# Input projections as seven-product Strassen blocks over even and odd tokens, and a 31-tap convolution as three half-rate filters, in a two-layer fp32 trunk

## The chip, the cores and the metric

One core of one Trainium2 chip runs the whole program. The metric is the device time of one execution in microseconds. The core's engines run side by side: TensorE (PE; its weight loads are shown as PEld), VectorE (DVE), ScalarE (ACT) and GpSimd (POOL). SyncE (SP) issues every transfer, in one queue, in the order in which the instructions stand there.

## What is computed

`SEQ` is 2048 tokens, `D_MODEL` 1024 channels, everything fp32. Layer 0 has mixer A, layer 1 mixer B.

```python
for l in range(DEPTH):                       # DEPTH = 2
    mod = cond @ ada_w[l] + ada_b[l]         # shift, scale, gate from silu(c)
    u = x * (1.0 + scale) + shift
    if l == 0:                               # mixer A
        a, g, z = split(u @ a_w_in + a_b_in, 3)           # 1024 -> 3072
        h = causal_depthwise_conv_31(a * sigmoid(g)) + a_conv_b
        h = silu(layer_norm_over_channels(h))
        y = (h * silu(z)) @ a_w_out + a_b_out
    else:                                    # mixer B
        bg, cg, v, z = split(u @ b_w_in, 4)               # 1024 -> 4096
        y = (bg * causal_depthwise_conv_3(cg * v) * silu(z)) @ b_w_out
    x = layer_norm(ALPHA * x + gate * y) * post_ln_g[l] + post_ln_b[l]
```

## The kernel before

**Tiling.** The tokens are four quarters of T = 512, the channels K = 8 blocks of 128. A projection's result is a PSUM bank of 128 channels by 512 tokens. Each fp32 product is made of three matmuls on rounded parts (hi by hi, hi by lo, lo by hi; L138 to L140 in `products`, L310 to L312 in `mixer_out`), so one output block of one quarter costs 8 x 3 matmuls. There are 24 such blocks for layer A's input projection, 32 for layer B's and 16 for the two output projections: 72 x 24 x 4 = 6912 matmuls of 512 columns. Beside them stand 416 128x128 transposes: of x on the way in (L168), of the convolution's result for its channel statistics (L511), and of layer A's output.

**Weights.** `weight` (L112) loads a block raw (512 KB, L83, on SP), ScalarE copies the hi part (L117), GpSimd subtracts to get the lo part (`wi_lo`, `wb_lo`, `wo_lo`, L119, 1024 elements a partition). This is done again for each of the four quarters. `fold_gate` (L246) multiplies the output weights by the gate row once (L271) and stores them (L272).

**Convolution.** `conv_a` (L389) works on one block of 128 channels and one quarter, as two chains of taps on VectorE, each with its own PSUM bank (`pca`, `pcb`; L412); the few leading taps are on ScalarE and GpSimd, L422 adds the chains. The taps stand in a list, `todo`, of which the main program issues some after every projection block.

**Layer B's middle.** `gated_b` (L595) multiplies two banks (L601), does the three taps (L607, L609), and gates (L611, L613).

**Order.** A table of numbers, `SCH`, sets how the quarters interleave: the projection of a quarter's layer B runs beside the statistics, the norm (`a_norm`, L548 to L555) and the output projection of the next quarter's layer A. The taps of the convolution are thus spread over about three quarters of the program. Inside what the numbers fix, a scheduler places instructions on each engine; matmuls of one block stay together. Of other lines that are named later, L218 sums the modulation rows from `ada_w`, L319 takes an output projection out of PSUM and adds the residual, L514 and L516 gather statistics, L456 is the GLU product on GpSimd, L455 copies a halo, and L464 stores z.

Of the kernel before, what the change touches and what calls it, by code (L numbers as in the profile page):

```python
# [9 lines left out]
F32 = mybir.dt.float32  # L10
# [9 lines left out]
K = D // P  # L20
T = 512
# [3 lines left out]
KB = 3  # L25
DEPTH = 2
ALPHA = (2.0 * DEPTH) ** 0.25
EPS = 1e-5
BOOST = 600
EXTRA = {3: (3,)}  # L30
BUFS = dict(raw=2, whi=3, wlo=3, uh=9, ul=9, xk=2, uf=2, big=28, h=5, ta=4, tv=5, zz=2, xr=4)
BANKS = dict(mm=4, tp=2, conv=2)
MAIN = ("raw", "whi", "wlo")
SPARE = ("raw", "xr", "xr")
SCH = dict(f0=4, p1=21, a1=5, n0=9, b0=20, bq=17, nq=10, pb=0, pa=16, ra=7, rb=4, rc=11, g0=3, w0=1, bt=600, ev=2, x4=3, io=0, c0=1, cq=0, pj=1, k1=1, k2=5, gb=0, gk=0, vv=0, a0=2, wm=0, rr=1, pk=6, ay=5, wq=1, lk=1, z1=3, zq=0, mo=0, m0=0)
# [3 lines left out]
def hybrid_trunk(ctx, tc, x, c, ada_w, ada_b, a_w_in, a_b_in, a_conv_w, a_conv_b,  # L39
                 a_ln_g, a_ln_b, a_w_out, a_b_out, b_w_in, b_conv_w, b_w_out,  # L40
                 post_ln_g, post_ln_b, out):
    nc = tc.nc
# [10 lines left out]
    def bank(tag, name):  # L53
        return psum.tile([P, T], F32, tag=tag, bufs=BANKS[tag], name=name)


# [5 lines left out]
    nc.gpsimd.memset(mhalf, -0.5)  # L62

    rows = []
# [9 lines left out]
              ("pg0", cols(post_ln_g[0]), K),  # L74
              ("pb0", cols(post_ln_b[0]), K),
# [3 lines left out]

    in_order = [bool(SCH["io"])]  # L80

    def load(dst, src):
        ins = nc.sync.dma_start(dst, src)  # L83
        if in_order[0]:
            tc.keep_in_program_order(ins)

    def load_columns(gi, g):
        n = sum(r[2] for r in g)
        rt = st("ta", [P, P], f"rt{gi}")
# [5 lines left out]
        nc.tensor.transpose(pt[:, :n], rt[:n, :], ident[:n, :n])  # L95
        ct = const.tile([P, n], F32, name=f"cols{gi}")
        nc.vector.tensor_copy(ct, pt[:, :n])
        o = 0
        for key, ap, m in g:
            col[key] = ct[:, o:o + m]  # L100
            o += m

    load_columns(0, first)
# [3 lines left out]
    def wa_col(k, e):  # L107
        i = k * K + e
        return col["wa0"][:, i:i + 1] if i < half else col["wa1"][:, i - half:i - half + 1]


    def weight(src, name, tags=MAIN):  # L112

        raw = st(tags[0], list(src.shape), name + "_raw")
        load(raw, src)
        hi = st(tags[1], list(src.shape), name + "_hi", F32R)
        nc.scalar.copy(hi, raw)  # L117
        lo = st(tags[2], list(src.shape), name + "_lo", F32R)
        nc.gpsimd.tensor_tensor(lo, raw, hi.bitcast(F32), op=ALU.subtract)  # L119
        return hi, lo  # L120

    def weight_in(w, m, e, name, **kw):
        o = m * D + e * P
        hi, lo = weight(w[:, o:o + P].rearrange("(k p) j -> p k j", p=P), name, **kw)
        return [hi[:, k] for k in range(K)], [lo[:, k] for k in range(K)]

    beside = deque()

    def products(pss, ws, acts):

        behind = None
        for k in range(K):
            ah, al = acts[k]
            with ExitStack() as order:
                if behind is not None:
                    order.enter_context(tc.issue_after(behind))
# [4 lines left out]
            behind = None  # L141
            if beside and len(pss) == 1 and k % SCH["ev"] == SCH["ev"] - 1:
                with tc.issue_after(mm.ins):
                    behind = beside.popleft()()

    def split(full, tagh, tagl, name, eng):
        hi = st(tagh, [P, T], name + "h", F32R)
        lo = st(tagl, [P, T], name + "l", F32R)
        nc.scalar.copy(hi, full)
        eng.tensor_tensor(lo, full, hi.bitcast(F32), op=ALU.subtract)  # L150
        return hi, lo

    su1 = const.tile([P, K], F32, name="su1")
    bu1 = const.tile([P, K], F32, name="bu1")

    w_dram = [dram.tile([2, K // 2, P, 2, T], F32, name="w_dram0"),
              dram.tile([2, K // 2, P, 2, T], F32, name="w_dram1")]
    z_dram = dram.tile([NQ, K, P, T], F32, name="z_dram")
    n_dram = dram.tile([S, D], F32, name="n_dram")

    def prep_k(q, l, k, src, su, bu, tag="xk"):

        xk = st(tag, [P, NT, P], f"xk{l}_{q}_{k}")
        load(
            xk, src[q * T:(q + 1) * T, k * P:(k + 1) * P].rearrange("(t p) j -> p t j", p=P))
        pt = bank("tp", f"ptx{l}_{q}_{k}")
        for t in range(NT):
            nc.tensor.transpose(pt[:, t * P:(t + 1) * P], xk[:, t, :], ident)  # L168
# [13 lines left out]
    def normalise(dst, src, rs, mv, name):  # L182
# [3 lines left out]
        for d, s in zip(dst, src):  # L186
            nc.scalar.activation(d, s, AF.Identity, scale=rs, bias=nb)

    def ada_sum(l, m, h, res, shared=0):

# [541 lines left out]
```

## Time and profile before

| what | value |
|---|---|
| time, median of 3 executions | 1740.15 us (1736.21 to 1741.71) |
| the profiled execution: its time, its span | 1741.81 us, 1740.0 us |
| TensorE busy | 1669.4 us, 96% of the span |
| VectorE busy | 1313.7 us, 76% |
| GpSimd busy | 1114.6 us, 64% |
| ScalarE busy | 636.1 us, 37% |
| moved by DMA | 265.27 MB, mean 152 GB/s |

The time is taken by the device; the span goes from the first to the last instruction of the profile. The shares are averages over stages that look different: VectorE, at 76% on average, is at 98% in some stretches. Mean durations hide a spread where an instruction waits for something inside itself, so three views are used: the groups of instructions by line with their mean, the single lines with minimum, median and maximum, and windows of time with the busy time of every engine.

### The profile page before, as it was taken

What the parts mean: (1) busy time and instruction counts of PE and PEld (TensorE: products, weight loads), DVE (VectorE), ACT (ScalarE), POOL (GpSimd) and SP (SyncE); (2) the same over time, 40 slices, a digit from 0 to 9 for tenths busy, and PEclk for the clock granted to TensorE, in tenths of its full rate; (3) what the DMA queues carried; (4) which work ended last, traced back from release to release, by engine and by line L of the source; (5) the groups of instructions that cost most, each with busy time, mean ns of one, the idle gap of its engine ahead of it and who ended that gap; (6) DMA issues with size and microseconds to landing.
All of it is one profiled execution on the core that took longest, in us unless ns stands there. A gap on an engine that the chain in (4) does not pass through costs nothing.

```text
span 1740.0 us, 20572 instructions
## 1 busy us (share of the span) xinstructions
PE 1669.4 (96%) x7468; PEld 1371.9 (79%) x7468; DVE 1313.7 (76%) x1748; ACT 636.1 (37%) x820; POOL 1114.6 (64%) x710
## 2 busy tenths in 40 slices
PE   6999899889999999999999999999999999999997
PEld 4788688677788787888888787888888778888886
DVE  8999999899996545899994736599995736444464
ACT  2444545534223442435322434344422414222221
POOL 3798558876775876656554857655644777654444
PEclk9999999889999999999999999999999999999999
DMA  9965435766653564533432554543333436443342
GB/s 253 292 208 184 125 99 188 262 215 176 219 192 116 175 214 125 168 115 113 115 97 85 176 183 150 173 124 109 103 97 98 145 109 219 125 137 97 97 140 82
DMA packets 332053, 265.27 MB, mean 152 GB/s; under 512 B 10536, under 2 KB 289456, under 8 KB 331952
## 3 DMA queue, kind: packets, MB, share of 16 engines
q1 hardware_dynamic: 331952, 263.96, 48.5%
q8 instruction: 59, 0.97, 0.2%
q14 instruction: 42, 0.34, 0.1%
HBM read 230.36 MB, written 33.55 MB: 152 GB/s over the span
## 4 chain that ended last, share of the span: by engine, by line
PE 72%; DVE 11%; POOL 5%; DMA 5%; issue 4%; ACT 2%; SPq 1%; POOLq 0%; DVEq 0%; ACTq 0%
PE pq L138 11%; PE pq L139 11%; PE pq L140 11%; PE pi L139 7%; PE pi L140 7%; PE pi L138 7%; PE po L311 5%; PE po L312 5%; PE po L310 5%; POOL wi_lo L119 1%; DVE pca L412 1%; DVE v L555 1%; DVE pcb L412 1%; PE ptx L168 1%; DVE acc L548 1%
## 5 line engine op out<-in xcount | busy, mean ns | idle before, releaser
L119 POOL TENSOR_TENSOR wb_lo<-wb_raw,wb_hi 128x1024 fp32r<-128x1024 f32 x128 | 312.6, 2445 | 202.1 <-ACT wb_hi L117 173.6
L119 POOL TENSOR_TENSOR wi_lo<-wi_raw,wi_hi 128x1024 fp32r<-128x1024 f32 x96 | 232.9, 2428 | 158.0 <-ACT wi_hi L117 147.5
L412 DVE SCALAR_TENSOR_TENSOR pca<-h,cols,pca 128x512 f32<-128x512 f32 x440 | 328.3, 746 | 1.3
L412 DVE SCALAR_TENSOR_TENSOR pcb<-h,cols,pcb 128x512 f32<-128x512 f32 x416 | 310.0, 745 | 25.5 <-ACT pcb L400 25.2
L117 ACT CAST wb_hi<-wb_raw 128x1024 fp32r<-128x1024 f32 x128 | 134.5, 1051 | 392.3 <-PE pq L139 217.4
L119 POOL TENSOR_TENSOR wo_lo<-wo_raw,wo_hi 128x1024 fp32r<-128x1024 f32 (+1 forms) x65 | 165.7, 2551 | 77.8 <-ACT wo_hi L117 68.5
L117 ACT CAST wi_hi<-wi_raw 128x1024 fp32r<-128x1024 f32 x96 | 100.5, 1048 | 237.6 <-PE pi L139 105.0
L319 DVE TENSOR_TENSOR r<-po,r 128x512 f32<-128x512 f32 x64 | 43.4, 681 | 187.0 <-PE po L312 186.9
L117 ACT CAST wo_hi<-wo_raw 128x1024 fp32r<-128x1024 f32 (+1 forms) x65 | 67.3, 1037 | 151.6 <-PE po L312 74.8
L609 DVE SCALAR_TENSOR_TENSOR cc<-hb,cols,cc 128x512 f32<-128x512 f32 x64 | 95.3, 1489 | 1.1
L601 DVE TENSOR_TENSOR hb<-pq,cv 128x512 f32<-128x512 f32 x32 | 21.9, 686 | 66.0 <-PE pq L140 63.4
L611 DVE TENSOR_TENSOR cc<-cc,szb 128x512 f32<-128x512 f32 x32 | 55.7, 1740 | 15.8 <-ACT szb L605 15.2
L168 PE MATMUL ptx<-ident,xk 128*128 128x128 f32 x256 | 40.3, 290 | 16.7 <-ACT uf L170 7.5
L168 PEld LDWEIGHTS ptx<-ident,xk 128*128 128x128 f32 x256 | 32.9, 150 | 24.4 <-ACT uf L170 8.1
L138 PE MATMUL pq<-u_0h,wb_hi 128*128 128x512 f32 x128 | 50.7, 396 | 0.7 <-ACT szb L605 0.7
L218 DVE SCALAR_TENSOR_TENSOR ada<-adaw,cond,ada 128x512 f32<-128x512 f32 x32 | 48.7, 1522 | 2.5 <-DMA adaw<-in_ada_w_dram 2.1
L140 PE MATMUL pq<-u_0h,wb_lo 128*128 128x512 f32 x128 | 50.4, 394 | 0.0
L139 PE MATMUL pq<-u_0l,wb_hi 128*128 128x512 f32 x128 | 50.4, 393 | 0.0
L138 PE MATMUL pq<-u_7h,wb_hi 128*128 128x512 f32 x128 | 50.3, 400 | 0.0
L139 PE MATMUL pq<-u_2l,wb_hi 128*128 128x512 f32 x128 | 50.1, 392 | 0.0
L139 PE MATMUL pq<-u_7l,wb_hi 128*128 128x512 f32 x128 | 50.1, 392 | 0.0
L138 PE MATMUL pq<-u_1h,wb_hi 128*128 128x512 f32 x128 | 50.1, 391 | 0.0
(373 smaller groups left out, 5086.7 us busy)
## 6 DMA issues: line engine op xcount, KB each, us to landing
wb_raw<-in_b_w_in_dram SPq DMA_DIRECT2D x128, 512.0 KB
wi_raw<-in_a_w_in_dram SPq DMA_DIRECT2D x96, 512.0 KB
wo_raw<-w_dram SPq DMA_DIRECT2D x63, 512.0 KB
adaw<-in_ada_w_dram SPq DMA_DIRECT2D x60, 256.0 KB
adak<-in_ada_w_dram SPq DMA_DIRECT2D x32, 256.0 KB
xk<-in_x_dram SPq DMA_DIRECT2D x32, 256.0 KB
z_dram<-zv SPq DMA_DIRECT2D x32, 256.0 KB
zz<-z_dram SPq DMA_DIRECT2D x32, 256.0 KB
```

The lines of the kernel that those rows point to most:

```text
L117: nc.scalar.copy(hi, raw)
L119: nc.gpsimd.tensor_tensor(lo, raw, hi.bitcast(F32), op=ALU.subtract)
L138: nc.tensor.matmul(ps, hi[k], ah, start=(k == 0), stop=False)
L139: nc.tensor.matmul(ps, hi[k], al, start=False, stop=False)
L140: mm = nc.tensor.matmul(ps, lo[k], ah, start=False, stop=(k == K - 1))
L168: nc.tensor.transpose(pt[:, t * P:(t + 1) * P], xk[:, t, :], ident)
L310: nc.tensor.matmul(pss[t], gh[:, sl], hi, start=(k == 0), stop=False)
L311: nc.tensor.matmul(pss[t], gh[:, sl], lo, start=False, stop=False)
L312: nc.tensor.matmul(pss[t], gl[:, sl], hi, start=False, stop=(k == K - 1))
L412: nc.vector.scalar_tensor_tensor(out=ts[dst], in0=h[:, k:k + T], scalar=wa_col(k, e), in1=ts[src], op0=ALU.mult, op1=ALU.add)
L609: nc.vector.scalar_tensor_tensor(out=cc, in0=hb[:, k:k + T], scalar=wbc(k), in1=cc, op0=ALU.mult, op1=ALU.add)
L611: nc.vector.tensor_tensor(cc, cc, sz, op=ALU.mult)
```

## The change

**Strassen blocks.** The two halves of the sequence (`sc` 0 and 1, 1024 tokens each) take the place of the quarters in both input projections. A half is seen as two streams of 512, the even and the odd tokens (`hf` 0 and 1); quarter q is now 2 x half + parity. A `Pair` takes two 128-wide output blocks, the four even and the four odd blocks of the contraction, and the two streams: a 2x2 by 2x2 block product, made with seven block products (`PARTS`) where eight stood. Each is 4 x 3 matmuls. They gather in three PSUM banks (x, y, z); the bank x runs through four of the parts and is read in between. Layer A has 12 pairs, layer B 16, each in two halves: (12 + 16) x 7 x 12 x 2 = 4704 matmuls, and with the 1536 of the output projections 6240.

**Sums around the products.** VectorE forms the differences of the streams (`u_second`, L220: t1 to t4, four subtractions for each pair of contraction blocks, and three of their four lo parts, L186). The weight sums `s` (L279 to L285) are on GpSimd for layer A and on VectorE for layer B. The banks leave PSUM through a ScalarE copy (L320, L322) followed by a VectorE addition (L326 or L328), three per pair.

**Weights once.** Every block is split into hi and lo in the first half only, now 512 elements a partition at a time (L186), stored (`kept`, 512 KB a part) and loaded again for the second half. `fold_gate` stores the output weights as hi and lo too, and the output projections load both.

**Convolution.** The 31 taps become three filters on streams of half the rate: 16 even taps on the even stream, 15 odd taps on the odd one, and 16 sums of taps on the sum of the streams. A unit is one channel block and one half (1024 tokens), so there are 16 units, each with 47 taps of 512 columns, three of them on ScalarE and GpSimd (`LEAD`), two started on ScalarE. The GLU products are on VectorE (L582, L588); its result, the convolution's result and z go through DRAM (`h_dram`, `acc_dram`, `z_dram`), as does layer B's gated product (`cc_dram`).

**Order.** All of layer A's input projection comes first (half 0, half 1), then output projections of quarters 0 and 1, layer B's first half, and so on. Three taps are issued per block product of an input projection and one per step of an output projection. TensorE's instructions keep program order; the additions that free a bank are marked urgent.

```diff
-                for ps, (hi, lo) in zip(pss, ws):
-                    nc.tensor.matmul(ps, hi[k], ah, start=(k == 0), stop=False)
-                    nc.tensor.matmul(ps, hi[k], al, start=False, stop=False)
-                    mm = nc.tensor.matmul(ps, lo[k], ah, start=False, stop=(k == K - 1))
...
+    def u_second(U, f0, f1, name):
+        (b11, b21), (b12, b22) = f0, f1
+        tt = lambda o, a, b: nc.vector.tensor_tensor(o, a, b, op=ALU.subtract)
+        with urgent():
+            tt(b11, b12, b11)
+            U["t1"].append(u_tile(b11, name + "t1", nc.vector))
+            U["b22"].append(u_tile(b22, name + "b22"))
...
+    PARTS = (1, 2, 5, 6, 3, 7, 4)
...
+            s = st("s", [P, KH, P], f"s{self.name}")
+            tt = self.adds.tensor_tensor
+            for n, p in enumerate(PARTS):
...
+                elif p == 5:
+                    tt(s, a21, a22, op=ALU.add)
+                elif p == 6:
+                    tt(s, s, a11, op=ALU.subtract)
+                elif p == 3:
+                    tt(s, a12, s, op=ALU.subtract)
+                elif p == 7:
+                    tt(a11, a11, a21, op=ALU.subtract)
+                    src = a11
+                else:
+                    src = a22
+                wt = st("w", [P, 2, KH, P], f"w{self.name}_{p}", F32R)
+                split(src, wt[:, 0], wt[:, 1])
+                store(keep[n], wt.bitcast(F32))
...
+        BANK = {1: "x", 6: "x", 7: "x", 4: "x", 2: "y", 5: "z", 3: "z"}
+        BLOCK = {1: "b11", 2: "b21", 3: "b22", 4: "t4", 5: "t1", 6: "t2", 7: "t3"}
...
+                if scale == 1.0:
+                    nc.vector.tensor_tensor(t[key], bk[b], t[key], op=ALU.add)
...
+                if p == 1:
+                    snap("c11", "x", scale, bias0)
+                elif p == 6:
+                    snap("c12", "x", scale, bias0)
+                elif p == 5:
+                    snap("c22", "z", 1.0, bias1)
+                elif p == 2:
+                    add("c11", "y", scale)
+                    self.after(self, "c11")
...
-        for k in range(1, lead):
-            part = st("tv", [P, T], f"part{q}_{e}_{k}")
...
+        even = lambda r: tiles["h"][:, 0, r:r + T]
+        odd = lambda r: tiles["h"][:, 1, r + 1:r + 1 + T]
+        both = lambda r: tiles["xs"][:, r:r + T]
...
+        def tap_e(r):
+            mac("a", even(r), w1[:, 2 * r, e:e + 1], "lead" if r == LEAD else "a")
...
+        def tap_o(r):
+            mac("b", odd(r), w1[:, 2 * r + 1, e:e + 1], "b")
...
+        def tap_s(r):
+            if r < R // 2:
+                mac("a", both(r), w2[:, r, e:e + 1], "a", ALU.subtract if r == 0 else ALU.add)
+            else:
+                mac("b", both(r), w2[:, r, e:e + 1], "b")
```

On VectorE before, in the middle of layer B's first projection, the taps of two convolution units of quarter 1 stand among the gating of one layer B block (`cc0_2`, `hb0_2`; names carry quarter and block):

```order
L607 TENSOR_SCALAR cc0_2_4135<-hb0_2_4083,cols1_198 128x512
L412 SCALAR_TENSOR_TENSOR pcb1_6_4031<-h1_6_2621,cols3_396,pcb1_6_4031 128x512
L412 SCALAR_TENSOR_TENSOR pca1_5_3878<-h1_5_2542,cols3_396,pca1_5_3878 128x512
L609 SCALAR_TENSOR_TENSOR cc0_2_4135<-hb0_2_4083,cols1_198,cc0_2_4135 128x512
L412 SCALAR_TENSOR_TENSOR pcb1_6_4031<-h1_6_2621,cols3_396,pcb1_6_4031 128x512
L422 TENSOR_TENSOR acc1_5_3880<-pca1_5_3878,acc1_5_3880 128x512
L609 SCALAR_TENSOR_TENSOR cc0_2_4135<-hb0_2_4083,cols1_198,cc0_2_4135 128x512
L412 SCALAR_TENSOR_TENSOR pca1_6_4030<-h1_6_2621,cols2_390,acc1_6_4032 128x512
L611 TENSOR_TENSOR cc0_2_4135<-cc0_2_4135,szb0_2_4133 128x512
```

In the changed kernel the same place on VectorE, layer B's first half (pairs `c2` and `b2`, the convolution unit `1_5`, weight sums of pair `b2`):

```order
L467 SCALAR_TENSOR_TENSOR pca1_5_7506<-xs1_5_7517,w2_88,pca1_5_7506 128x512
L326 TENSOR_TENSOR c22c2_0_7278<-pxc2_0_7182,c22c2_0_7278 128x512
L467 SCALAR_TENSOR_TENSOR pca1_5_7506<-xs1_5_7517,w2_88,pca1_5_7506 128x512
L281 TENSOR_TENSOR sb2_0_7375<-sb2_0_7375,rawb2_0_0_7371 128x512
L285 TENSOR_TENSOR rawb2_0_0_7371<-rawb2_0_0_7371,rawb2_0_1_7373 128x4x128
L326 TENSOR_TENSOR c11b2_0_7392<-pyb2_0_7426,c11b2_0_7392 128x512
L796 TENSOR_TENSOR hb0c2_0_7490<-pxc2_0_7182,c11c2_0_7205 128x512
L283 TENSOR_TENSOR sb2_0_7375<-rawb2_0_0_7371,sb2_0_7375 128x512
L786 SCALAR_TENSOR_TENSOR ccc2_0_0_7496<-hb1c2_0_7415,second_columns_77,ccc2_0_0_7496 128x512
```

Between the taps stand now the weight sums (both operands in SBUF) and the additions that empty banks (one operand a PSUM bank `px`, `py`), and TensorE waits for the latter when a bank comes round again.

On SP before, early in layer A's second quarter, three weight loads among stores of z and of the folded output weights:

```order
L464 DMA z_dram_88<-zv0_5_1367 128x512
L272 DMA w_dram0_86<-wf0_1_7_1523 128x512
L83 DMA wi0_7_1_raw_1565<-in_a_w_in_dram 128x8x128
L83 DMA wi0_7_2_raw_1612<-in_a_w_in_dram 128x8x128
L83 DMA wi1_0_2_raw_1760<-in_a_w_in_dram 128x8x128
L272 DMA w_dram0_86<-wf0_1_6_1470 128x512
L464 DMA z_dram_88<-zv0_6_1505 128x512
```

On SP in the changed kernel, in layer A's first half, loads of raw weights among stores of split weights (`kepta2_0`, part by part), of z and of the convolution's result:

```order
L71 DMA rawa3_0_1_1241<-in_a_w_in_dram 128x8x128
L74 DMA kepta2_0_1059<-wa2_0_6_1178 128x1024
L74 DMA z_dram_97<-c22z0_0_980 128x512
L74 DMA kepta2_0_1059<-wa2_0_3_1217 128x1024
L74 DMA kepta3_0_1238<-wa3_0_1_1244 128x1024
L74 DMA acc_dram_98<-acc00_0_1055 128x512
L74 DMA z_dram_97<-c21z0_0_1171 128x512
L74 DMA kepta2_0_1059<-wa2_0_7_1276 128x1024
L71 DMA rawz2_0_0_1421<-in_a_w_in_dram 128x8x128
```

A raw load now stands behind stores that wait for VectorE (`acc_dram`) and GpSimd (`kept`). In all, SP issues 1148 transfers in the changed kernel and 666 before; by their sizes 470 MB and 264 MB.

## Rows read from the trace of the kernel before

**Rows 1.** Page: span, busy time of each engine, share of the span, instructions.
```profile
span 1740.0 us, 20572 instructions
PE 1669.4 (96%) x7468; PEld 1371.9 (79%) x7468; DVE 1313.7 (76%) x1748; ACT 636.1 (37%) x820; POOL 1114.6 (64%) x710
```

**Rows 2.** Windows: stretch, length, busy of PE, PEld, DVE, ACT, POOL (instructions), clock, DMA, GB/s.
```profile
core 0: us, PE busy (x) PEld busy (x) DVE busy (x) ACT busy (x) POOL busy (x), PEclk, DMA share, GB/s
0.00:40.00 40.00, 23.19 (x86) 18.18 (x87) 31.89 (x79) 11.26 (x14) 15.70 (x22) 0.91 0.97 251
200.00:300.00 100.00, 100.00 (x465) 82.80 (x464) 98.35 (x145) 47.22 (x65) 66.28 (x44) 1.00 0.40 127
800.00:900.00 100.00, 100.00 (x449) 82.76 (x448) 97.90 (x133) 39.09 (x53) 56.28 (x39) 1.00 0.36 104
900.00:1000.00 100.00, 97.26 (x449) 79.78 (x448) 64.31 (x62) 33.82 (x45) 66.36 (x40) 0.98 0.42 129
1000.00:1100.00 100.00, 98.75 (x447) 81.53 (x446) 42.75 (x53) 34.63 (x42) 65.18 (x37) 1.00 0.48 158
1600.00:1700.00 100.00, 100.00 (x443) 82.78 (x442) 50.56 (x37) 25.05 (x30) 46.75 (x23) 1.00 0.36 116
1700.00:1740.00 40.00, 28.49 (x126) 23.27 (x124) 20.70 (x31) 4.07 (x5) 17.03 (x14) 0.90 0.22 79
```

**Rows 3.** Lines by shape, VectorE operations with a PSUM operand: busy, mean ns, idle before.
```profile
L412 DVE SCALAR_TENSOR_TENSOR pca<-h,cols,pca 128x512 f32<-128x512 f32 x440 | 328.3, 746 | 1.3
L319 DVE TENSOR_TENSOR r<-po,r 128x512 f32<-128x512 f32 x64 | 43.4, 681 | 187.0 <-PE po L312 186.9
L514 DVE BATCH_NORM_STATS2 s<-pl 128x6 f32<-128x512 f32 x32 | 22.1, 690 | 25.0 <-PE pl L511 24.9
L516 DVE BATCH_NORM_AGGREGATE mv<-s 128x2 f32<-128x12 f32 x16 | 3.3, 206 | 0.4
```

**Rows 4.** Lines by shape, VectorE operations whose two inputs are in SBUF.
```profile
L609 DVE SCALAR_TENSOR_TENSOR cc<-hb,cols,cc 128x512 f32<-128x512 f32 x64 | 95.3, 1489 | 1.1
L611 DVE TENSOR_TENSOR cc<-cc,szb 128x512 f32<-128x512 f32 x32 | 55.7, 1740 | 15.8 <-ACT szb L605 15.2
L555 DVE TENSOR_TENSOR v<-v,zz 128x512 f32<-128x512 f32 x32 | 41.1, 1293 | 4.7 <-DMA zz<-z_dram 4.7
L218 DVE SCALAR_TENSOR_TENSOR ada<-adaw,cond,ada 128x512 f32<-128x512 f32 x32 | 48.7, 1522 | 2.5 <-DMA adaw<-in_ada_w_dram 2.1
```

**Rows 5.** Single lines: count, minimum/median/maximum ns, first to last start (us).
```profile
L609 DVE SCALAR_TENSOR_TENSOR cc<-hb,cols,cc x64: 735/752/2914, 426.7 to 1681.1; 128x512 f32<-128x512 f32 x64
L555 DVE TENSOR_TENSOR v<-v,zz x32: 674/1143/2864, 275.6 to 1388.3; 128x512 f32<-128x512 f32 x32
L570 DVE TENSOR_TENSOR r<-r,g0row x16: 1212/1408/3427, 642.7 to 1689.5; 128x1024 f32<-128x1024 f32 x16
L271 POOL TENSOR_TENSOR wf<-wf,grow x32: 1268/1293/1756, 85.9 to 527.5; 128x512 f32<-128x512 f32 x32
```

**Rows 6.** Lines by shape, GpSimd operations, and TensorE's transposes of x.
```profile
L119 POOL TENSOR_TENSOR wb_lo<-wb_raw,wb_hi 128x1024 fp32r<-128x1024 f32 x128 | 312.6, 2445 | 202.1 <-ACT wb_hi L117 173.6 <-PE pq L139 19.9 <-PE pq L140 3.8
L456 POOL TENSOR_TENSOR h<-av,sg 128x512 f32<-128x512 f32 x32 | 42.7, 1336 | 0.0
L455 POOL COPY h<-halo 128x30 f32<-128x30 f32 x32 | 11.9, 381 | 15.9 <-DVE cc L609 9.3 <-DVE pca L412 6.6
L168 PEld LDWEIGHTS ptx<-ident,xk 128*128 128x128 f32 x256 | 32.9, 150 | 24.4 <-ACT uf L170 8.1 <-DVE pca L412 5.6 <-DMA xk<-in_x_dram 4.1
```

**Rows 7.** Page: mean GB/s of the DMA in 40 equal slices; and the window 0 to 100.
```profile
GB/s 253 292 208 184 125 99 188 262 215 176 219 192 116 175 214 125 168 115 113 115 97 85 176 183 150 173 124 109 103 97 98 145 109 219 125 137 97 97 140 82
DMA packets 39386, 25.30 MB, mean 253 GB/s; under 512 B 1416, under 2 KB 35794, under 8 KB 39378
```

**Rows 8.** Waits: SP's queue, by releaser: sum in us, count, longest.
```profile
SPq L83 <- POOL wb_lo L119: 464.7, 109, 14.0
```

**Rows 9.** Waits of TensorE: the largest sum.
```profile
PE ptx L168 <- ACT uf L170: 7.5, 2, 7.0
```

More of the change, by code (lines that the diff above doesn't have):

```diff
@@ L146, in split @@
[L146 to L157, printed above, removed]
@@ new lines, in product, with order_of @@
+    def product(pair, p, ks=range(KH)):
+        for i in ks:
+            pair.mm(p, i)
+            if i == KH - 1:
+                pair.evacuate(p)
+    def order_of(n, first=0):
+        seq = []
+        for p in range(first, n - 1):
+            last = p + 1 == n - 1
+            seq += [(p, 3), (p + 1, 1), (p, 7), (p + 1, 2), (p + 1, 5)]
+            seq += [(p + 1, 6), (p, 4)] if last else [(p, 4), (p + 1, 6)]
+        return seq + [(n - 1, 7), (n - 1, 3), (n - 1, 4)]
+    mod0 = const.tile([P, KH, 2, 2], F32, name="mod0")
@@ new lines, in hybrid_trunk, with begin_out, wait @@
+    for r, ks in ((5, (0, 1)), (1, (2,)), (2, (2,)), (5, (2,)), (1, (3,)), (2, (3,)), (5, (3,))):
+        product(pa[1][0], r, ks)
+    norms = {q: a_norm(q, gs[0, q]) for q in range(NQ)}
+    fu = {}
+    outs = {}
+    def begin_out(q, l, rows):
+        if l == 0:
+            fu[q] = [st("u", [P, T], f"ub{q}_{k}") for k in range(K)]
+        outs[l, q] = mixer_out(q, l, gs[l, q], rows, fu.get(q))
+        next(outs[l, q])
+    def wait(n, gen):
+        for _ in range(n):
+            yield
+        yield from gen
@@ new lines, in hybrid_trunk @@
+    run_out(0, 0, wait(3, norms[1]))
+    begin_out(1, 0, rows)
+    run_out(0, 1, wait(7, join_first(0)))
+    pb = pairs_b(0, US[1, 0])
+    n_b = len(pb)
+    start = [(0, 1), (0, 2), (1, 1), (1, 2), (0, 5), (0, 6), (0, 3), (0, 7), (1, 5), (0, 4), (1, 6)]
+    for pair in pb:
+        pair.adds = nc.vector
+    back = background_b()
+    for n, (p, r) in enumerate(start + order_of(n_b, 1)):
+        if n == 4:
+            join(0)
+        product(pb[p], r)
+        tick(RATE["b"], *([back] if n > 8 else ()))
@@ new lines, in hybrid_trunk @@
+    for _ in back:
+        pass
+    need(2)
+    begin_out(0, 1, out_rows(0, 1))
+    b_gate(0, gs[1, 0])
+    run_out(1, 0, wait(3, norms[2]))
+    need(3)
+    rows = out_rows(2, 0)
+    begin_out(2, 0, rows)
+    run_out(0, 2, wait(3, norms[3]))
+    begin_out(3, 0, rows)
+    b_gate(1, gs[1, 1])
+    run_out(0, 3, wait(7, join_first(1)))
+    begin_out(1, 1, out_rows(1, 1))
+    run_out(1, 1)
+    join(1)
+    pb = pairs_b(1, US[1, 1])
+    for p, r in start + order_of(n_b, 1):
+        product(pb[p], r)
+        tick(0)
@@ L709 @@
+    rows = out_rows(2, 1)
+    for q in (2, 3):
+        begin_out(q, 1, rows)
+        b_gate(q, gs[1, q])
+        run_out(1, q)
 _INS = ["x", "c", "ada_w", "ada_b", "a_w_in", "a_b_in", "a_conv_w", "a_conv_b", "a_ln_g", "a_ln_b",
```

1170 lines of the change are left out of this document (658 added, 512 removed).

## The prediction

> **What bounds the kernel now.** I read the page first: TensorE is busy 1669.4 of 1740.0 us, VectorE 1313.7, GpSimd 1114.6 [rows 1]. Then the waits of TensorE: the largest sum is 7.5 us [rows 9], so nothing but its own work holds it up. Then windows of 100 us, because an average over stages hides what the next bound would be. In the middle of the program TensorE is busy for 100 of 100 us with some 450 matmuls, and in two of those windows VectorE stands at 98.35 and 97.90 [rows 2]: there it is full as well, with TensorE only just ahead of it. In 1600 to 1700 VectorE is at 50.56. So the kernel is bound by TensorE everywhere, and by VectorE almost as much wherever there are convolution taps. A change that takes work off TensorE gains in the stretches without taps; in those with taps the gain is what VectorE allows. I therefore cost the change as two stretches in a row, one of VectorE and one of TensorE.
>
> **TensorE.** The changed kernel has 6240 matmuls of 512 columns instead of 6912. In 1600 to 1700 TensorE ran 443 in 100 us, 0.2257 us each [rows 2]. The 672 saved are 152 us at this price. That is the most the change can save; 416 transposes are as before, at 0.150 each by their weight load [rows 6], and 144 one-column matmuls take no more than that each.
>
> **Where VectorE's stretch ends.** In the changed kernel all of layer A's projection comes first, and taps are issued at three per block product, so the 16 units run on into the middle of layer B's first half. I counted what stands on VectorE up to the convolution's last operation (L520 of the unit 1_7), by kind, and priced each kind:
> - 720 taps and alike with a PSUM operand, 0.746 [rows 3]: 537 us.
> - 166 additions and statistics of 512 columns with a PSUM operand, at 0.681 (L319; L514 has 690) [rows 3]: 113 us.
> - 116 statistics over 128 columns. There is no row for this shape. L570 has 512 columns more than L555 and a minimum 538 ns longer [rows 5], 1.05 ns a column; 0.690 less 384 columns is 0.287: 33 us.
> - 49 small ones at 0.206 [rows 3]: 10 us.
> - 229 with both inputs in SBUF: the weight sums of layer B, the stream differences of `u_second` and their lo parts, GLU products, the norm, layer B's taps and gates.
>
> The last price is the one that decides. The four lines of that kind before have means of 1489, 1740, 1293 and 1522 ns, weighted 1.505 [rows 4]. Yet the minima are 735 and 674, the maxima 2914 and 2864 [rows 5]; L609's median of 752 says that most run unhindered and some take 2.2 us more. That excess is about one GpSimd subtraction of 1024 columns, 2.445 us [rows 6]: such an operation seems to wait inside itself for a GpSimd operation that has begun. In the changed kernel these are of 512 columns, 1.336 us by L456 [rows 6], 0.55 of the length. Own time 0.71 (mean of the minima by kind), mean excess 0.79 at 1.505; 0.79 x 0.55 = 0.43, so I take 1.145: 262 us. The lower bound is 0.71 (no GpSimd operation in the way), the upper 1.505 (the excess doesn't shrink).
>
> VectorE's stretch: 537 + 113 + 33 + 10 + 262 = 955 us.
>
> [...]
>
> **What lies around it.**
> - Start: the first bank can't be read before the modulation weights and x are in: 4 x (8 x 256 KB + 2 x 512 KB), two weight blocks and the first stores, about 16 MB. The first 100 us before moved 253 GB/s, and the slice behind the first 292 [rows 7]; so about 60 us. VectorE has 38 us of its tally in that time: 22 idle.
> - In layer A's first half the taps have only begun. From the first reading of a bank to that half's end I count 160 us on VectorE beside 175 of TensorE (759 matmuls, 24 transposes): 15 idle.
> - A full VectorE is at 97.90 to 98.35 of 100 [rows 2]: 2% of 955, 19.
>
> Then TensorE: behind the point where the last convolution operation stands, 2941 matmuls x 0.2257 and 92 transposes x 0.150 are left: 678 us. At the borders between stages I add 12: the windows 900 to 1000 and 1000 to 1100, with output projections, lose 2.74 and 1.25 [rows 2], some 4 us for two of these, and six are left. The end costs 11.5, as in 1700 to 1740, where TensorE is busy 28.49 of 40 [rows 2].
>
> 22 + 955 + 15 + 19 + 678 + 12 + 11.5 = 1712.5 us of span. The profiled execution took 1741.81 with a span of 1740.0; adding the 1.8 gives **1714**. That execution is 1.7 above the median of the runs, 1740.15, a difference that is smaller than the 0.3% (some 5 us) that a measurement of this kernel can tell from no change.
>
> **Costed at nothing**, and by what cover: ScalarE's copies (1136 instructions for 820, the weights' ones half as long; it is at 37% [rows 1]). The transfers: 470 MB instead of 264. Over 1712 us that is 275 GB/s as a mean, just under the best slice, 292 [rows 7]; but the split weights stored and loaded again (103 MB each) and the 67 MB of output weights can run ahead only as far as the buffers go (`w` has 5). If that cover is gone, the stage concerned takes its bytes over 292. SP's queue: a raw weight's load now stands behind stores which wait for VectorE and GpSimd. Before, SP already waited 464.7 us for GpSimd in L83 alone [rows 8] without TensorE waiting. A stall of that wait's maximum, 14.0, for each of 28 pairs would be 392 us; none costs 0. I take none: the raw loads in the order shown stand a pair ahead.
>
> **The rivals.**
> 1. *GpSimd and VectorE shut each other out, and layer B's first half becomes the bound (slower).* L609 shows VectorE waiting inside an operation; L271 on GpSimd, 1268 at the least and 1756 at the most [rows 5], shows it the other way round. If no two-input operation of VectorE overlaps GpSimd, their times add: in that half GpSimd has 215 operations of 512 columns x 1.293 (L271's median) + 37 small x 0.381 [rows 6] = 292, VectorE 127 two-input ones x 0.71 = 90; 382 us. My sum has 345 there for VectorE (338 and 2%), TensorE needs 314. That is 37 more, **1751**. It decides as soon as that stage takes over 375 us. The DMA stands close behind: the stage moves 103 MB, 353 us at 292 GB/s, and at 253 it would be 407, 62 above 345, for 1776. For it: 292 us of GpSimd in a stage of 345. Against it: 193 of VectorE's 338 us are operations with a PSUM operand, beside which nothing in the rows shows GpSimd waiting. [...]
> 2. *The two-input operations cost their own 0.71 (faster by much).* The lo parts are then rarely in the way, as for the median of L609. 229 x 0.433 x 1.02 = 101 less: **1613**. TensorE's own floor lies below: 6240 x 0.2257 + 560 x 0.150 = 1492, and with 23 idle at the start, 12, 11.5 and 1.8 it is 1540. Against it: the means of all four lines.
> 3. *The excess doesn't shrink with the GpSimd operation's length:* 1.505, 229 x 0.36 x 1.02 = 84 more: **1798**. For it: there are more GpSimd operations than before, and L611's mean is 1740. Against it: L609's maximum is a minimum plus one operation of 2.4 us.
>
> **How the numbers follow.** Chances: my sum 0.47, rival 1 0.28, rival 2 0.15, rival 3 0.10. The likeliest gives 1714, and its own range is 1680 to 1745 (start and borders off by 20, the two-input price by 0.1 either way). The range of all is 1615 to 1795: above 1613 lies about half of rival 2, and half of rival 3 lies within. Faster by over 0.3% (below 1735): 0.40 of my case, 0.15, and 0.02 of rival 1, 0.57. Within 0.3%: 0.05, 0.04 of rival 1, 0.01 of rival 3, 0.10. Slower: 0.02, 0.22, 0.09, 0.33.
>
> **What the changed profile would show.** Right: VectorE near 98% from about 200 us to the convolution's end at about 1010 us, TensorE at some 80% there, then near 100%; TensorE's largest waits on L80 for the additions L326 and L328; the two-input lines at a mean of 1.1 to 1.2, with maxima near 2.1. Rival 1: TensorE waits for weights (`w`, released by GpSimd's L186 or by DMA) in layer B's first half, GpSimd near full there, L186 well over 1.34 us. Rival 2: means near 0.75, the convolution done before 920. Rival 3: means near 1.5. Wrong altogether: TensorE waiting on loads of `raw` or `kept` with VectorE idle, which would mean that SP's queue or the DMA is the bound; or TensorE's clock, 1.00 in the full windows now [rows 2], falling in the stretch in which it waits.

## The result, and the profile after

| | kernel before | changed kernel |
|---|---|---|
| time, median | 1738.49 us | 1823.17 us (1821.89 to 1828.44) |
| ratio to before, 95% interval | 1 | 1.0491 (1.0463 to 1.0520) |
| span of the profiled execution | 1740.0 us | 1820.1 us |
| mean granted clock of TensorE | 0.982 | 0.941 |

The change made the kernel 4.9% slower; 1714 had been predicted, with a range of 1615 to 1795. The median before is here that of four executions, the 1740.15 above that of three. The page of the changed kernel, span and busy times, answers to [rows 1]:

```profile
span 1820.1 us, 21371 instructions
PE 1602.8 (88%) x6956; PEld 1303.9 (72%) x6956; DVE 1161.4 (64%) x1737; ACT 662.3 (36%) x1134; POOL 1001.6 (55%) x868
```

TensorE is busy 67 us less, not 152, and stands idle for 217 us instead of 71 (span less busy time in both). No engine is fuller than before. The windows view, cut at the stages of TensorE's program (start; the rest of layer A's first half; its second half; output projections of quarters 0 and 1; layer B's first half; four output projections; layer B's second half; the last two), columns as in [rows 2]:

```profile
core 0: us, PE busy (x) PEld busy (x) DVE busy (x) ACT busy (x) POOL busy (x), PEclk, DMA share, GB/s
0.00:106.60 106.60, 75.91 (x358) 69.74 (x359) 34.80 (x49) 31.80 (x53) 37.19 (x37) 0.84 0.53 166
106.60:357.00 250.40, 236.84 (x1056) 194.01 (x1056) 217.75 (x335) 125.69 (x214) 199.70 (x161) 0.97 0.83 289
357.00:651.30 294.30, 255.75 (x1109) 209.21 (x1108) 229.53 (x383) 122.08 (x194) 149.90 (x124) 0.92 0.86 308
651.30:773.80 122.50, 102.06 (x442) 82.11 (x440) 95.53 (x155) 50.54 (x91) 71.57 (x63) 0.93 0.74 251
773.80:1187.60 413.80, 343.70 (x1423) 268.93 (x1422) 320.16 (x440) 172.35 (x309) 315.09 (x265) 0.92 0.72 252
1187.60:1394.70 207.10, 190.40 (x850) 153.17 (x849) 125.36 (x183) 80.82 (x153) 115.40 (x99) 0.98 0.86 300
1394.70:1711.30 316.60, 307.89 (x1345) 254.14 (x1344) 87.75 (x125) 60.48 (x98) 68.54 (x82) 0.98 0.65 210
1711.30:1820.10 108.80, 90.25 (x384) 72.56 (x384) 50.47 (x72) 18.57 (x27) 44.18 (x41) 0.93 0.68 249
```

Layer B's two halves run the same 1344 matmuls. The second takes 316.6 us, the first 413.8, and in the first VectorE is busy 77% of the time, GpSimd 76%, TensorE 83%: no engine is full, and each waits for another. The waits of TensorE in the changed kernel, in us, count and longest (before: [rows 9]):

```profile
PE pmb L80 <- POOL ada L412: 22.2, 3, 9.3
PE pxc L80 <- ACT wc L185: 20.2, 3, 9.3
PE pm L80 <- DMA adak<-in_ada_w_dram: 19.6, 3, 9.7
PE po L80 <- DVE r L728: 14.1, 10, 5.5
PE ptxua L83 <- ACT ufua L209: 13.2, 8, 7.0
```

Three names head the list, each from another stage: layer B's modulation sums (`pmb`, layer A's second half), the first part of a pair in layer B's first half (`pxc`), the modulation of layer A at the start (`pm`). None of these three is an addition that empties a bank; the first of that kind stands fourth (L728, in the output projections), and L326, which the prediction named, has 7.5 us at `pzc` as its largest.

### The profile page after: what moved, and what is told of

Read it like the earlier page. It is cut to its first block, busy times and chain, and to the rows that moved or that the text cites. A ratio compares the mean times of both kernels' runs of the same rounds, so it can differ in the third digit from the quotient of the medians.

```text
span 1820.1 us, 21371 instructions
## 1 busy us (share of the span) xinstructions
PE 1602.8 (88%) x6956; PEld 1303.9 (72%) x6956; DVE 1161.4 (64%) x1737; ACT 662.3 (36%) x1134; POOL 1001.6 (55%) x868
## 4 chain that ended last, share of the span: by engine, by line
PE 49%; DVE 18%; DMA 13%; POOL 10%; issue 6%; ACT 3%; SPq 1%; POOLq 0%; DVEq 0%; ACTq 0%
PE po L80 9%; PE pxc L80 7%; PE pxb L80 6%; PE pxa L80 6%; DVE pca L467 4%; PE pzc L80 4%; PE pzb L80 3%; PE pza L80 3%; DVE pcb L467 3%; PE pxz L80 2%; PE pm L80 2%; PE pya L80 2%; PE pyb L80 1%; PE pyc L80 1%; DMA wr<-w_dram 1%
## 5 line engine op out<-in xcount | busy, mean ns | idle before, releaser
L467 DVE SCALAR_TENSOR_TENSOR pcb<-h,w,pcb 128x512 f32<-128x512 f32 x224 | 166.7, 744 | 6.6 <-ACT pcb L475 6.4
L467 DVE SCALAR_TENSOR_TENSOR pca<-h,w,pca 128x512 f32<-128x512 f32 x192 | 142.9, 744 | 0.2
L467 DVE SCALAR_TENSOR_TENSOR pca<-xs,w,pca 128x512 f32<-128x512 f32 x128 | 95.6, 746 | 0.3
L728 DVE TENSOR_TENSOR r<-po,r 128x512 f32<-128x512 f32 x64 | 43.2, 679 | 80.0 <-issue 33.0
L467 DVE SCALAR_TENSOR_TENSOR pcd<-xs,w,pcd 128x512 f32<-128x512 f32 x112 | 83.5, 745 | 3.1 <-ACT pcd L509 3.1
L706 ACT ACTIVATE r<-r,nb,rs 128x512 f32<-128x512 f32 x64 | 47.7, 807 | 90.0 <-DVE nb L701 90.0
L412 POOL TENSOR_TENSOR ada<-ada,adaw 128x512 f32<-128x512 f32 x48 | 64.9, 1354 | 12.0 <-ACT adaw L406 10.2
L80 PE MATMUL pm<-cond,adak 128*128 128x1 f32 x256 | 49.0, 327 | 19.6 <-DMA adak<-in_ada_w_dram 19.6
L80 PEld LDWEIGHTS pm<-cond,adak 128*128 128x128 f32 x256 | 48.9, 298 | 20.3 <-DVE ua00t L220 10.1
L186 POOL TENSOR_TENSOR wa<-rawa,wa 128x512 fp32r<-128x512 f32 x32 | 42.1, 1322 | 28.0 <-ACT wa L185 28.0
L707 POOL TENSOR_TENSOR r<-r,g 128x512 f32<-128x512 f32 x32 | 49.8, 1566 | 3.9 <-ACT r L706 3.9
L186 POOL TENSOR_TENSOR wc<-rawc,wc 128x512 fp32r<-128x512 f32 x32 | 43.5, 1360 | 13.0 <-ACT wc L185 12.6
L186 POOL TENSOR_TENSOR wb<-rawb,wb 128x512 fp32r<-128x512 f32 x32 | 43.1, 1347 | 11.9 <-ACT wb L185 11.9
L708 POOL TENSOR_TENSOR r<-r,b 128x512 f32<-128x512 f32 x32 | 47.7, 1499 | 0.6
L186 POOL TENSOR_TENSOR wf<-wf 128x512 fp32r<-128x512 f32 x32 | 43.9, 1377 | 6.2 <-ACT wf L185 6.2
```

Of the source, the lines that this page charges most:

```text
L80: return tc.keep_in_program_order(nc.tensor.matmul(*args, **kw))
L186: (eng or nc.gpsimd).tensor_tensor(lo, src, hi.bitcast(F32), op=ALU.subtract)
L412: nc.gpsimd.tensor_tensor(acc, acc, raw[:, j], op=ALU.add)
L467: nc.vector.scalar_tensor_tensor(out=tiles[out], in0=src, scalar=w, in1=tiles[acc], op0=ALU.mult, op1=op)
L706: nc.scalar.activation(r, r, AF.Identity, scale=rs, bias=nb)
L707: eng.tensor_tensor(r, r, g[h], op=ALU.mult)
```

## The experiments

Differences are against the changed kernel's 1823; ratios are against the kernel before. Theories: A, what comes late in an in-order queue (SP's loads behind stores, TensorE's program) stops TensorE; B, the prediction's, VectorE is full up to the convolution's end; C, the DMA's bandwidth; D and E, GpSimd, by exclusion with VectorE or by its load; F, the chain of weight sums; G, the folding's transfers.

**Half of the taps.** In `tap_e`, `tap_o` and `tap_s`:

```diff
         def tap_o(r):
+            if r % 2:
+                return
...
```

> Leaves out 21 of the 42 taps that each convolution unit has on VectorE besides its first ones (the odd ones), 336 instructions of 0.745 us, 250 us of VectorE's work; the convolution is incomplete. Theory B, the prediction's step (VectorE full up to the convolution's end): that stretch shrinks by 100 us or more, to about 1700. Theory A (stalls in the order of SP's queue and of TensorE's program): VectorE is only 80% busy there and its taps are mostly not what TensorE waits for; 0 to 40 us less.

The time is 1806.86 us, 16 less, ratio 1.0390 (1.0362 to 1.0418). Layer A's second half and layer B's first half with half of the taps, from the windows view:

```profile
352.80:649.20 296.40, 257.26 (x1110) 209.89 (x1109) 155.89 (x257) 123.94 (x196) 147.93 (x124) 0.91 0.85 308
760.40:1169.00 408.60, 347.35 (x1422) 275.26 (x1421) 263.36 (x356) 172.37 (x309) 313.00 (x265) 0.90 0.73 256
```

VectorE loses 74 and 57 us of work there, and the stages take 296 and 409 us as against 294 and 414. Theory B is out: VectorE isn't what these stages wait for.

**Stores on another queue, and hardly any stores.** The first puts the stores of split and folded weights on ScalarE's queue; in the second only the first pair of each layer stores.

```diff
-                store(keep[n], wt.bitcast(F32))
+                nc.scalar.dma_start(keep[n], wt.bitcast(F32))
...
```

> The stores of the split weights (kept) and of the folded output weights go out on ScalarE's queue instead of SP's; everything else as in the changed kernel (1823 us). Theory A, SP's single queue: loads stand behind stores that wait for GpSimd, TensorE stalls for weights in layer B's first half (70 us idle there) and at the start; so 30 to 60 us less, SP's waits of L74 for GpSimd gone, layer B's first half at 350 to 380 us instead of 414. Theory B, VectorE is the bound up to the convolution's end as the prediction had it: within 10 us of 1823. Theory C, the DMA's bandwidth: the bytes are the same, within 10 us of 1823. Theory D, GpSimd and VectorE shut each other out: no change either.

> Only the first pair of each layer stores its split weights, 14 stores instead of 196; the second half's pairs all load these, so the loads are as many and as large as before and the second half computes with the wrong weights. Theory A (SP's queue): as in the run with the stores on ScalarE's queue, 30 to 60 us less. Theory C (bandwidth): 96 MB less of 470, at 259 GB/s some 370 us of transfers less, all of it in the two first halves; 60 us less or more, and clearly more than with the stores moved to the other queue. Theory B (VectorE): within 10 us of 1823.

They take 1835.41 us (ratio 1.0558), 12 more, and 1811.62 (1.0421), 12 less. In its strong form theory A, that the stores of split weights in SP's queue hold up what TensorE needs, is out: with 182 of them gone layer B's first half still takes 407 us, and its DMA moves 122 GB/s where it moved 252. So theory C is out for that stage too. Both kernels still store the folded output weights, and single stalls do hang on these stores. The chain of waits in the changed kernel around one of the longest (start, us, what):

```profile
1003.19 1.75 POOL wf L186
1004.94 0.02 issue
1004.96 2.65 DMA w_dram<-wf
1007.60 0.02 issue
1007.62 4.15 DMA rawc<-in_b_w_in_dram
```

and TensorE there (start, us, instruction, idle before it):

```profile
1012.46 0.80 PE L80 MATMUL pxc<-ub00b11h,wc 128*128 128x512 f32 x1 [9.28 <-ACT wc L185]
...
1014.41 0.63 PE L80 MATMUL pxc<-ub01b11h,wc 128*128 128x512 f32 x1
1014.83 0.63 PE L80 MATMUL pxc<-ub01b11l,wc 128*128 128x512 f32 x1
1015.26 0.63 PE L80 MATMUL pxc<-ub01b11h,wc 128*128 128x512 f32 x1
```

GpSimd finishes the lo part of a folded weight, SP stores it, and the load of the next pair's raw weights starts 0.02 us after this store has landed; TensorE has waited 9.28 us. It is not the order in SP's queue that it waits for: at 1015.45 us SP issues a load 0.43 us after it has begun to issue a store. It waits for its buffer, since the folded weights `wf` and the raw weights take turns in the same four `raw` buffers. SP's waits of this kind in layer B's first half, in the changed kernel and with the stores on ScalarE's queue (sum in us, count, longest):

```profile
SPq L71 <- DMA w_dram<-wf: 20.4, 11, 4.1
```
```profile
SPq L71 <- DMA w_dram<-wf: 66.0, 13, 16.8
```

So moving the stores to another queue did not free the loads of them, and made these waits longer.

Behind the stop at 1012 us matmuls start 0.42 to 0.43 us apart, 1.9 times the 0.2257 of [rows 2]; the granted clock of this stretch is 0.51, where it is 1.00 in 1600 to 1700 there (columns as in [rows 2]):

```profile
1012.40:1016.60 4.20, 4.01 (x9) 2.73 (x10) 1.51 (x1) 2.04 (x5) 4.11 (x3) 0.51 0.66 245
```

By the starts of the records 161 matmuls of the changed kernel lie so far apart, nearly all behind a stop (154 within 20 matmuls of a distance of over 1 us between two starts): 161 x 0.2 = 32 us that no row of waits shows. In the kernel before, counted in the same way, it is 74 matmuls, 15 us. Behind most of the long stops the trace shows some 5 to 8 such matmuls, 1 to 1.6 us.

**GpSimd's load in layer B's first half.** Three kernels: the weight sums back on GpSimd; the gate sums and the folding of layer B left out, with layer A's folded weights in their place; the folding's transfers kept, but GpSimd's 46 operations left out or copied on ScalarE.

```diff
-    for pair in pb:
-        pair.adds = nc.vector
```
```diff
-    back = background_b()
+    back = iter(())
...
```
```diff
...
+            else:
+                nc.scalar.copy(wr[:, 0], w[:, 1])
+                nc.scalar.copy(wr[:, 1], w[:, 1])
```

> Layer B's weight sums go back to GpSimd, 64 operations of 512 elements: 1.29 us each, 83 us more on GpSimd and some 73 less on VectorE. Theory D (GpSimd and VectorE shut each other out, GpSimd decides layer B's first half): 40 us or more longer. Theory B (VectorE decides): 30 to 70 us shorter. Theory A (late weights): longer by 10 to 40, since each sum takes longer on GpSimd and the parts come later, with no stall of VectorE gained.

> Leaves out the sums of layer B's gate and the folding of its output weights, which lie beside layer B's first half; the output projections of layer B load those of layer A instead (as many bytes). It takes 46 GpSimd operations of 1.3 us and 8 MB of stores and as many loads from SP's queue and from the four raw buffers that this stage shares. Theory E (GpSimd's throughput): some 60 us less, that stage at about 355. Theory F (chain of sums): 10 to 25 less, by shorter queues on GpSimd and SP. Theory B (VectorE): no change.

> Layer B's gate sums and the folding of its output weights stay beside layer B's first half with all their loads, stores, buffers and ScalarE scalings, but without GpSimd: the 14 additions are left out and the 32 products and lo parts become copies on ScalarE (the values of layer B's output weights are wrong). Theory E (GpSimd's operations are what that stage pays for): as with the folding left out, the stage at 350 to 365 us, 50 to 65 us less in all. Theory G (the folding's transfers, through SP's queue and the four raw buffers, hold up the raw weights): within 15 us of the changed kernel's 1823.

They take 1847.77 us (ratio 1.0631), 25 more; 1763.76 (1.0139), 59 less; and 1793.61 (1.0311), 30 less. The first is what theory A forecast, against B and D; the third lies between the forecasts of E and G. Layer B's first half in the three, in this order (the first profile is of an execution 11 us above its median):

```profile
780.30:1224.00 443.70, 358.27 (x1423) 277.14 (x1422) 267.58 (x377) 173.00 (x309) 378.99 (x328) 0.88 0.67 234
```
```profile
775.20:1130.30 355.10, 326.65 (x1419) 265.45 (x1418) 301.85 (x438) 152.20 (x277) 248.41 (x217) 0.95 0.70 246
```
```profile
775.00:1157.70 382.70, 335.23 (x1424) 266.27 (x1422) 309.51 (x440) 182.69 (x327) 252.58 (x219) 0.94 0.78 273
```

GpSimd's busy time 379, 315, 253, 248 goes with 444, 414, 383, 355 us. The folding costs 59 us, about half of it (31 in this stage) by GpSimd's operations, the rest (28) with its transfers and ScalarE's part. No run takes this rest apart, but the traces show a wait that goes with it. For raw weights ScalarE and VectorE wait 50 us in this stage of the changed kernel, 21 us without GpSimd's part of the folding, and in no row without the folding. SP's wait for a `raw` buffer that holds a folded weight, 20.4 us above, is this without GpSimd's part, and is in no row without the folding:

```profile
SPq L71 <- DMA w_dram<-wf: 5.8, 6, 1.7
```

GpSimd is not full in any of the four; it is a link that each part of a weight passes, and what is queued there delays it. Whether one of its operations costs by its own length, by holding a `raw` buffer longer, or by the operations of VectorE that wait for it (VectorE's busy time fell from 320 to 310 us with the same 440 instructions), these runs don't separate. So between D and E nothing is decided.

**The chain of sums.** Each sum written over an operand that is spent, so that it needn't wait for the split of the one before:

```diff
...
-                    tt(s, s, a11, op=ALU.subtract)
+                    tt(a11, a11, a21, op=ALU.subtract)
+                    tt(a21, a22, a11, op=ALU.subtract)
+                    src = a21
...
```

> The four weight sums of a pair keep their number and engine, but each is written over an operand that is no longer needed, so that a sum does not wait until ScalarE and GpSimd have split the one before it. Theory F (the chain sum, hi part, lo part, next sum through three engines with a single tile s bounds layer B's first half): 20 to 50 us less, that stage at 365 to 395 us instead of 414. Theory E (GpSimd's throughput or the two engines' exclusion): within 8 us of the changed kernel's 1823.

It takes 1828.99 us (ratio 1.0511), 6 more, with layer B's first half at 413: theory F is out.

**Layer A's second half.** One kernel loads only every other part of the split weights there, one leaves out the four modulation sums of layer B.

```diff
+                    if n % 2 == 0 or self.key[0] not in "az":
                         wt = st("w", [P, 2, KH, P], f"w{self.name}_{p}", F32R)
                         load(wt.bitcast(F32), kept[self.key][n])
```
```diff
-        modulation_b(0, 0, res[1, 0, 0])
...
```

> In layer A's second half only every other part of the split weights is loaded, the part behind it uses the same tile (wrong values, 48 loads of 512 KB and 25 MB fewer, all else equal). Theory C for this stage (the DMA, 308 GB/s there and 395 in its fullest slice, delivers the background's data too late): layer A's second half at 255 to 270 us instead of 294, 25 to 40 us less in all. Theory A (TensorE's order): within 8 us of 1823.

> Leaves out the four modulation sums of layer B on TensorE (16 one-column matmuls and their waits; the sums of the rows before them stay, layer B's scale and shift become constants). Theory A (they stop TensorE's program 22 us, and each stop is followed by some 6 to 8 matmuls at half clock, 1.5 us): 22 to 30 us less, all in layer A's second half. Theory C or E (TensorE then waits for the next late thing in this stage): less than 10.

They take 1801.52 us (ratio 1.0355), 22 less, and 1797.52 (1.0333), 26 less. The stage in the first (this profile is of an execution 10 us below its median) and in the second:

```profile
353.80:620.40 266.60, 250.31 (x1110) 205.84 (x1109) 224.19 (x374) 120.00 (x193) 152.18 (x124) 0.96 0.75 263
```
```profile
356.40:622.80 266.40, 248.02 (x1078) 201.63 (x1077) 231.01 (x379) 120.65 (x194) 147.60 (x124) 0.96 0.93 339
```

Both come to about 266 us from 294, by two ways; TensorE's wait in `pmb`, 22.2 us, is 4.6 in the first and gone in the second. So it is one stall: four small sums stand in TensorE's program, the rows that they need arrive late because split weights are loaded beside them, and TensorE stops. The four loads of rows before the longest wait (9.3 us, at 488.5) were issued from 461.9 us on and landed, where the trace tells it, after 7.3 and 9.0 us; with half of the split weights one of these four landed after 4.8. Bandwidth alone is not the bound, since without the sums the stage moves 339 GB/s and runs as fast.

**The start.** The modulation sums on VectorE, the first stores behind the start's loads, and in a second kernel each block's sum one block ahead in the program:

```diff
...
+                    else:
+                        nc.vector.scalar_tensor_tensor(out=acc[:, m], in0=raw[:, j], scalar=cj,
+                                                       in1=acc[:, m], op0=ALU.mult, op1=ALU.add)
...
```

> TensorE's and SP's order at the start and in layer A's second half: the modulation sums on VectorE with one matmul for each column instead of eight (224 one-column matrices fewer records), the first pair's early stores behind the start's loads by an explicit order, the tap tables in a free tile, and the four later modulation sums seven steps later in TensorE's program. Theory A (the start is TensorE's one-column matmuls and the transfers held up): the first bank is read at 65 to 80 us instead of 106.6, layer A's second half loses its 22 us of waits, 40 to 60 us less in all. If what is saved comes back as later stalls: less than 20.

> Modulation sums on VectorE as in the run with the start's order changed, and each block's sum in the program one block ahead of the transposes and stream differences that need it. Theory A (the start is a chain that each of the four blocks runs through from load to products, one after the other): overlapping two blocks brings the first bank to 75 to 85 us from 106.6, 20 to 30 us less in all. If the start is bound by VectorE or the DMA instead, the first bank stays at 95 to 105.

They take 1824.90 us (ratio 1.0489), 2 more, with the first bank at 101.9, and 1814.59 (1.0435), 9 less, with the first bank at 96.8. Kernels whose start is that of the changed kernel read it at 102.8 to 107.4, so the first has gained little or nothing. Its longest wait shows where the work went:

```profile
PE pm L81 <- DVE adacc L398: 61.4, 8, 19.7
```

TensorE now waits for VectorE, which does the sums between the stream differences. Only some 10 of the 47 us by which the start is longer than predicted could be broken off. An earlier kernel that only moved stores and the later sums took 1820.87 us, 2 less where 30 to 45 had been expected: the stall of the four sums moved to another place (one of 21.2 us). With the sums written over their operands besides it took 1829.02, 6 more where 50 to 90 less had been expected.

**Moving instead of leaving out.** 

> The sums of layer B's gate and the folding of its output weights move from layer B's first half to layer A's second half, behind that stage's own background work, where GpSimd is busy 150 of 294 us. Theory E (the stall is GpSimd's load in one stage, and can be moved to where GpSimd has time): layer B's first half at about 355, layer A's second half 0 to 20 longer, 35 to 55 us less in all. If the work costs as much wherever it stands: no change.

It takes 1791.99 us (ratio 1.0305), 31 less: layer B's first half is at 356.5, but layer A's second half is 12 and the output projections behind it 13 us longer. Combined with the start's edits and the later sums delayed by seven steps it is 1788.00 (1.0276; 1715 to 1750 had been expected), with the start one block ahead 1776.55 (1.0205; 1755 to 1770 expected). This is the fastest that computes everything, still 2% slower than the kernel before.

**The three places together.**

> The three places together: layer B's gate sums and folding left out, layer B's modulation matmuls left out, the start one block ahead. If they are separate causes: 59 + 26 + 8 = 93 us less, 1725 to 1740, about the kernel before. If they share a cause, clearly over 1750.

> As the run before, and half of the convolution's taps left out (250 us of VectorE's work). If VectorE is the next bound behind the three places (theory B, second in line): 40 us or more below the run before. If what is left is TensorE's own work and its stops: as in the run with half the taps alone, 10 to 20 us less.

The first takes 1722.99 us, ratio 0.9906 (0.9881 to 0.9932), 100 less, as against 59 + 26 + 9 = 94 singly: separate causes, and they add. It leaves work out, so it shows what the three places cost and is no faster kernel. With half of the taps gone too it is 1703.57 (0.9793), 19 less. The two stages without the three places, and then with half of the taps besides:

```profile
347.40:613.70 266.30, 247.42 (x1077) 201.09 (x1076) 235.16 (x383) 121.29 (x195) 149.54 (x124) 0.96 0.93 341
734.40:1088.80 354.40, 324.50 (x1420) 264.00 (x1419) 301.46 (x438) 152.11 (x277) 248.12 (x217) 0.95 0.70 246
```
```profile
350.20:608.70 258.50, 245.19 (x1077) 200.15 (x1076) 157.98 (x252) 121.92 (x194) 148.22 (x123) 0.97 0.95 351
718.20:1065.50 347.30, 324.33 (x1419) 264.50 (x1418) 250.11 (x354) 154.51 (x277) 252.72 (x217) 0.95 0.72 252
```

Taking 77 and 51 us from VectorE gives back 8 and 7. Even second in line VectorE is not the bound.

## Why the prediction was wrong

| stretch | predicted | measured |
|---|---|---|
| to the first reading of a bank | 60 | 106.6 |
| from there to the convolution's last operation (1079.5 us) | 951 | 972.9 |
| behind it (678 + 12 + 11.5) | 701.5 | 740.6 |

**The step that failed** is the model: "I therefore cost the change as two stretches in a row, one of VectorE and one of TensorE", with 955 us of VectorE work at 98%. VectorE was busy only 840 us up to the convolution's end and stood idle 240, where the sum had 56 (22 + 15 + 19). I had read from [rows 2] that a full VectorE reaches 98%, and concluded that it would be full wherever it had taps. The runs show in its place that TensorE stops at three places for things that are late, and that what makes them late isn't VectorE: 250 us of taps gave 16. In layer B's first half each part of a weight passes the DMA, ScalarE and GpSimd, four parts of seven VectorE as well, before TensorE, whose order is fixed, may go on; the stops add up while VectorE and GpSimd are busy three quarters of the time, and a sum by the fullest engine can't see them. Without the three places the kernel is at 1723, near the predicted 1714, but not in the way predicted: half of the taps less then gives 19 us.

**The price of VectorE's work** was too high, which hid the failure. Up to the convolution's end the sum had 115 us too much of VectorE's work and 184 us too little of its idle time. That only 69 us show, 47 of them in the start and 22 behind it, is luck. With the measured 840 the same sum would have given about 1600, still further off. The durations of VectorE's 1279 instructions up to there add up to 934 us, close to the 955, but they overlap. Taps in the changed kernel (start, us):

```profile
986.51 0.75 DVE L467 SCALAR_TENSOR_TENSOR pca<-xs,w,pca 128x512 f32<-128x512 f32 x1
987.17 0.75 DVE L467 SCALAR_TENSOR_TENSOR pcd<-xs,w,pcd 128x512 f32<-128x512 f32 x1
```

They start 0.66 us apart and last 0.75. The mean of [rows 3] counts the overlap twice: 720 x 0.09 = 62 us. The disputed two-input price, 1.145 predicted, was 1.05 over the 212 such operations up to the convolution's end (229 in the sum). So the scaling of the excess with GpSimd's operation was about right, and rivals 2 and 3, with 0.71 and 1.505, were wrong. The border within the middle stretch was wrong too: 759 matmuls behind the first reading is not the end of layer A's first half, which has 12 x 84 - 36 = 972 there. VectorE was idle for 33 of these 250 us, not 15.

**The start, "about 60 us"**, was mis-sized by 47. I took only the bytes. TensorE's chain in the changed kernel (start, us, what, count):

```profile
12.59 13.87 PE L80 MATMUL pm<-cond,adak 128*128 128x1 f32 x64 [9.57 <-DMA adak<-in_ada_w_dram]
...
41.01 2.71 PE L80 MATMUL pm<-cond,adak 128*128 128x1 f32 x12 [9.73 <-DMA adak<-in_ada_w_dram]
44.00 11.25 PE L80 MATMUL pm<-cond,adak 128*128 128x1 f32 x52 [0.28 <-DMA adak<-in_ada_w_dram]
```

Each block's 64 records of one column take 9.4 to 14.0 us, 49 in all, where I had 144 matmuls that "take no more than that each", 0.150, though in the kernel before the weight load alone of such a record took 0.191 to 0.248 on average; and four blocks follow each other. The bytes were not the limit: the DMA's share in the start is 0.53.

**Behind the convolution** TensorE was busy for 696 of 740 us, where the sum had 678 and 23.5 of idle time. No experiment takes these 39 us apart.

**"Costed at nothing": SP's queue.** Neither moving the stores of split weights nor taking them away gave more than 12 us. The stall at 1003 us is of another kind: loads wait for `raw` buffers that the folding holds, and what the prediction said of buffers was about `w` alone. What I didn't cost at all was TensorE's program order: four small sums in it cost 26.

**Rival 1** named the right stage, an engine that counts there, and the right sign. Of its signs one came, TensorE waiting for weights in that stage; GpSimd is not near full (76%), and its L186 takes 1.33 to 1.44 us, not well over 1.34. Its size was too small (1751), and its sum of the two engines is not what the stage takes: by the union of the records a GpSimd operation of 512 columns or a two-input operation of VectorE runs for 347 of 413.8 us. The trace does show operations of both engines that last longer than others of their line: the sums of L281 in this stage last 0.68 us at the least and 1.78 at the most, and over the minimum of their line GpSimd's operations of 512 columns spend 29 us there and VectorE's two-input ones 57. All 62 of these two-input ones that last over 1 us overlap an operation of GpSimd; of the 66 that last under 0.76 us 28 do. But the stage is not this alone, since in 67 us of it neither runs.

What stays open: how the folding's 59 us divide among GpSimd's time, the `raw` buffers and ScalarE, some 37 us of the start, and the 39 us behind the convolution.

## What to carry to other kernels

Before costing a restructured kernel by its fullest engine, follow one item (here a part of a weight) through all engines, count what stands in front of it in each queue, and ask who else uses its buffers: here a chain with its engines at 75 to 85% took longer (413.8 us) than the fullest of them had work (343.7). Fewer matmuls only pay where their operands are ready in time: here 672 fewer came with 85 us more. A stop of TensorE cost its length here, the 22.2 us in `pmb` with what came behind them 26, and behind most long stops some 5 to 8 matmuls started 0.42 to 0.43 us apart. To price work on an engine in a full stretch, take the distance between starts (0.66 us for the taps here), not the mean duration (0.75).

## What was not expected of the hardware

In this trace fp32 matmuls of one column are dear. The group of the start's modulation in the changed kernel (busy, mean ns, idle before), and the window of the first block (columns as in [rows 2]):

```profile
L80 PE MATMUL pm<-cond,adak 128*128 128x1 f32 x256 | 49.0, 327 | 19.6 <-DMA adak<-in_ada_w_dram 19.6
```
```profile
12.50:26.50 14.00, 13.91 (x65) 13.93 (x66) 0.00 (x1) 1.14 (x2) 2.77 (x3) 1.00 0.91 277
```

256 records stand for 128 instructions. One record takes 49.0 / 256 = 0.19 us on average, nearly as much as a matmul of 512 columns in the rounded type (0.2257), and one instruction twice that. The weight loads (PEld) are busy for 13.93 of 14.00 us in this window, the matmuls (PE) for 13.91; that the loads and not the single column fill the time is an estimate from this, which no run tests.
